# A hybrid pooling and delta-rule decoder trunk on one core: decays made from gate sums that are read back from DRAM, convolution states turned four chunks at a time, queries squared by token

## The chip, the cores and the metric

The kernel runs on one core of a Trainium2 chip, as one launch. The core has a matrix engine (TensorE, PE in the profile; PEld is its loading of weights), a vector engine (VectorE, DVE), a scalar engine (ScalarE, ACT), GpSimd (POOL), and a sync engine (SyncE, SP) that here issues all DMAs. Each engine runs its own instructions in the order in which the program gives them; between engines they wait on semaphores. The metric is the time of one execution in device microseconds; lower is better. The median of three runs counts.

## The reference

Two layers run on a prompt of 512 tokens and on 8 sequences of 8 new tokens (the samples), 576 tokens of 1024 channels in all. Layer 0 mixes tokens by pooling, layer 1 by a gated delta rule; each is followed by a SwiGLU feed-forward block. The change touches the delta-rule mixer alone:

```python
def short_conv(u, buf, w):
    up = jnp.concatenate([buf.astype(u.dtype), u], axis=1)
    out = up[:, 0:L] * w[0]
    for tap in range(1, CONV_WIDTH):
        out = out + up[:, tap:tap + L] * w[tap]
    return jax.nn.silu(out), up[:, L:]
...
    gc = jnp.cumsum(g, axis=-1)
    causal = idx[:, None] >= idx[None, :]
    decay = jnp.exp(jnp.where(causal, gc[..., :, None] - gc[..., None, :], -jnp.inf))
    a_mat = jnp.where(strict, jnp.einsum('bhnid,bhnjd->bhnij', kb, k) * decay, 0.0)
...
    qk = jnp.einsum('bhnid,bhnjd->bhnij', q, k) * decay
...
    q = l2norm(qkv_c[..., :GDN_QK_DIM].reshape(B, L, GDN_K_HEADS, GDN_HEAD_K)) * (GDN_HEAD_K ** -0.5)
    k = l2norm(qkv_c[..., GDN_QK_DIM:2 * GDN_QK_DIM].reshape(B, L, GDN_K_HEADS, GDN_HEAD_K))
```

For each of 16 value heads there is a gate g per token. Its running sum gc inside a chunk gives the decay between two tokens, exp(gc_i - gc_j) for i not before j, and nothing otherwise. Queries and keys (8 heads each, every one shared by two value heads) are scaled by the inverse root of their sum of squares. The convolution takes the last three rows of its input from a state, and gives the last three back as the new state.

## The kernel before

Activations lie with channels on the 128 partitions and tokens along the free dimension; the 576 tokens are handled as halves of 256 and 320. A product with a weight is done in three parts (mm3): weight and activation are split into a rounded part (H, h) and a rest (L, l), and TensorE sums wh x aH, wh x aL and wl x aH. A weight tile comes by DMA into one of three raw buffers (wraw), ScalarE makes wh, and VectorE (or POOL) makes wl.

The prompt is cut into four spans (SPANS) of 128 tokens, and the delta rule works span by span. The 16 value heads are done in four groups G of four. project(G) makes the group's inputs: eight chunks of 128 channels (two of keys, two of queries, four of values), each multiplied by the weights into the banks ps_m, convolved over time (ac, u) and passed through Silu; finish() then turns keys and values to tokens-first with transposes on TensorE, through the single bank ps_x. core(G) makes the decays (QD), the matrices Uw from keys and decays, inverts their 32x32 blocks by a long row of small VectorE products (inv32, tiles ia and ii), combines them, and scans over the spans (scan), braided with the samples' heads (sample_heads). QD has one buffer, so that of group G+1 can be written only when the last matmul of group G's scan has read it. gates(), run once in project(0), makes g for all heads, its split gH and gL, and exponentials of its sums (gce, kde, glp, gls). zproj, zgate and out0 make the output gate and the first half of the output projection, and fill gaps of the groups.

The program is not run in the order in which it is written. The class Plan records all operations with what each depends on, gives each a cost by engine and shape, and searches an order for each engine with a list scheduler, forwards and backwards, in ROUNDS rounds with random stirring from SEED. Operations given to EITHER may go to VectorE or POOL. The scheduler also puts in idle matmuls (ps_w) where it expects TensorE to wait. What it finds is the order in which each engine's instructions are issued; the kernel does not reorder at run time. All DMAs stand in SP's one order, too, and a DMA whose condition is not met holds those behind it.

The decays before, in core(G): for each span, EITHER multiplies the triangle t_le (128x128) by gH and by gL of four heads, into gts (128 x 512 each); TensorE multiplies both by the strict triangle t_gt_r into ps_s, which gives the differences of gate sums; ScalarE takes the exponential of 512 columns into QD; and EITHER multiplies by t_le, to clear the upper part. The squares before: keys are turned to tokens-first and squared on ScalarE with a sum over the free dimension (ksq); queries are squared channels-first in one instruction of 512 columns into u, and TensorE sums each span's 128 columns over the channels with a product by a column of ones. The convolution state before: 24 rows (8 sequences x 3) of four chunks come by DMA, and TensorE transposes each chunk by itself (crow, 24x24; nct on the way back, 27 rows).

## Time and profile before

| What | us |
| --- | --- |
| Median of 3 runs | 1647.77 (1647.66 to 1648.63) |
| The profiled execution | 1655.15 |
| Its span, first to last instruction | 1653.1 |
| TensorE busy in the span | 1610.3 |
| VectorE busy in the span | 1002.9 |
| ScalarE busy in the span | 690.7 |

The profile is of one execution, which took 7.4 us more than the median. Its times are counted from the first instruction. Busy time of an engine is the union of its instructions; on TensorE the instructions overlap, so a matmul's duration is longer than its share of the engine. The delta-rule layer lies about between 500 and 1150 us; before it are the pooling layer and its feed-forward block, behind it the rest of the output projection and the second feed-forward block. A line of a group names engine, operation, output and inputs with shapes; all recorded operations have line 283, so tiles are told apart by their names.

### The profile page before, as it was taken

What the parts mean: (1) busy time and instruction counts of PE and PEld (TensorE: products, weight loads), DVE (VectorE), ACT (ScalarE), POOL (GpSimd) and SP (SyncE); (2) the same over time, 40 slices, a digit from 0 to 9 for tenths busy, and PEclk for the clock granted to TensorE, in tenths of its full rate; (3) what the DMA queues carried; (4) which work ended last, traced back from release to release, by engine and by line L of the source; (5) the groups of instructions that cost most, each with busy time, mean ns of one, the idle gap of its engine ahead of it and who ended that gap; (6) DMA issues with size and microseconds to landing.
All of it is one profiled execution on the core that took longest, in us unless ns stands there. A gap on an engine that the chain in (4) does not pass through costs nothing. (4 is left out here: it accounts for less than half of the span.)

```text
span 1653.1 us, 30697 instructions
## 1 busy us (share of the span) xinstructions
PE 1610.3 (97%) x12421; PEld 1549.2 (94%) x12421; DVE 1002.9 (61%) x2085; ACT 690.7 (42%) x1431; POOL 116.8 (7%) x254
## 2 busy tenths in 40 slices
PE   8999999999999999999999999899999999999998
PEld 8999999999999998898898889789999999999997
DVE  6684213332487898998999899557685312233345
ACT  6654223212355945353463544424464322222244
POOL 4000000000000010021220121100000000000000
PEclk8899999999999999999999999999999999999999
DMA  6245223222366433324333323466644323222333
GB/s 175 74 142 156 78 77 90 88 79 77 93 176 164 119 87 87 100 73 128 96 91 106 109 72 113 159 176 198 203 142 141 90 80 94 78 72 75 101 112 114
DMA packets 329813, 185.27 MB, mean 112 GB/s; under 512 B 12235, under 2 KB 324140, under 8 KB 329407
## 3 DMA queue, kind: packets, MB, share of 16 engines
q1 hardware_dynamic: 329671, 183.30, 38.2%
q8 instruction: 98, 1.61, 0.4%
q14 instruction: 44, 0.36, 0.1%
HBM read 157.73 MB, written 25.77 MB: 111 GB/s over the span
## 5 line engine op out<-in xcount | busy, mean ns | idle before, releaser
L283 DVE TENSOR_TENSOR wl<-wraw,wh 128x1024 fp32r<-128x1024 f32 (+2 forms) x251 | 297.9, 1193 | 279.9 <-PE ps_B L283 88.9
L283 ACT ACTIVATE wh<-wraw 128x1024 fp32r<-128x1024 f32 (+2 forms) x259 | 265.7, 1034 | 470.2 <-PE ps_B L283 212.0
L283 PE MATMUL ps_m<-hH,wh 128*128 128x320 f32 (+1 forms) x832 | 249.1, 312 | 2.1 <-ACT hH L283 0.8
L283 PE MATMUL ps_m<-hL,wh 128*128 128x320 f32 (+1 forms) x832 | 245.4, 307 | 0.0
L283 PE MATMUL ps_m<-hH,wl 128*128 128x320 f32 (+1 forms) x832 | 243.5, 307 | 0.0
L283 PE MATMUL ps_B<-hH,wh 128*128 128x320 f32 x768 | 224.6, 312 | 0.1
L283 PE MATMUL ps_B<-hL,wh 128*128 128x320 f32 x768 | 222.4, 311 | 0.1
L283 PE MATMUL ps_B<-hH,wl 128*128 128x320 f32 x768 | 222.2, 312 | 0.0
L283 PE MATMUL ps_A<-hH,wl 128*128 128x256 f32 x768 | 204.3, 284 | 0.4 <-DVE wl L283 0.2
L283 PE MATMUL ps_A<-hH,wh 128*128 128x256 f32 x768 | 203.4, 284 | 1.2 <-DVE yo L283 1.2
L283 PE MATMUL ps_A<-hL,wh 128*128 128x256 f32 x768 | 203.5, 283 | 0.0
L283 PEld LDWEIGHTS ps_m<-hH,wh 128*128 128x128 f32 x832 | 155.1, 190 | 9.2 <-issue 1.9
L283 PEld LDWEIGHTS ps_m<-hH,wl 128*128 128x128 f32 x832 | 154.6, 190 | 3.8 <-issue 2.0
L283 PEld LDWEIGHTS ps_m<-hL,wh 128*128 128x128 f32 x832 | 155.5, 190 | 2.0
L283 PEld LDWEIGHTS ps_A<-hH,wh 128*128 128x128 f32 x768 | 141.2, 190 | 1.8 <-issue 1.4
L283 PEld LDWEIGHTS ps_A<-hH,wl 128*128 128x128 f32 x768 | 141.4, 190 | 1.4 <-DVE wl L283 1.0
L283 PEld LDWEIGHTS ps_B<-hH,wh 128*128 128x128 f32 x768 | 141.2, 189 | 0.9 <-ACT hH L283 0.3
L283 PEld LDWEIGHTS ps_A<-hL,wh 128*128 128x128 f32 x768 | 141.6, 190 | 0.4 <-DVE hL L283 0.4
L283 PEld LDWEIGHTS ps_B<-hL,wh 128*128 128x128 f32 x768 | 140.7, 189 | 0.4 <-DVE hL L283 0.3
L283 PEld LDWEIGHTS ps_B<-hH,wl 128*128 128x128 f32 x768 | 140.2, 189 | 0.4
L283 PE MATMUL ps_B<-aH,wh 128*128 128x320 f32 x352 | 104.0, 312 | 0.1
L283 PE MATMUL ps_B<-aL,wh 128*128 128x320 f32 x352 | 103.6, 310 | 0.0
(387 smaller groups left out, 3063.1 us busy)
## 6 DMA issues: line engine op xcount, KB each, us to landing
wraw<-in_ffn_w_in_dram SPq DMA_DIRECT2D x112, 512.0 KB
wraw<-in_gdn_w_in_dram SPq DMA_DIRECT2D x56, 512.0 KB
wraw<-in_ffn_w_out_dram SPq DMA_DIRECT2D x48, 448.0 KB
wraw<-in_gdn_w_out_dram SPq DMA_DIRECT2D x24, 512.0 KB
wraw<-in_ffn_w_out_dram SPq DMA_DIRECT2D x16, 512.0 KB
St<-in_state_gdn_rec_dram SPq DMA_DIRECT2D x32, 256.0 KB
out_dram<-St SPq DMA_DIRECT2D x32, 256.0 KB
z_d<-zz SPq DMA_DIRECT2D x16, 288.0 KB
```

The lines of the kernel that those rows point to most:

```text
L283: calls[e](*a, **k)
```

## The change

Four things change.

1. **Decays.** gates() sums the gate along each span for all 16 heads at once, heads on partitions (four matmuls of g with t_le into 16 x 512), copies it (gcr) and stores it to DRAM (gc_d, 32 KB). Per group and span, one DMA reads four heads' rows of it back to all 128 partitions (256 KB into QD); EITHER adds bar, which is -1e30 in the strict triangle and 0 elsewhere; and ScalarE takes four exponentials of 128 columns, one per head, with the negative gate sum of the partition's own token (ngs) as bias. The gts products of the spans, their matmuls and the product with t_le go; gH and gL stay for the samples alone (64 x 16).
2. **Queries squared by token.** Queries are transposed on TensorE like keys, and ScalarE squares each span with a sum into ksq, straight from PSUM. The column sums with ones stay for the samples alone (sqs).
3. **Convolution states.** The 24 rows of four chunks are put below each other on 96 partitions, by four DMAs, and turned with one transpose; on the way back four chunks of 27 rows are turned at once into 108 partitions, and each chunk is stored by two DMAs.
4. **The search.** ROUNDS goes from 46 to 40 and SEED from 4 to 2, and a constant of the cost of small matmuls from 3.2 to 3.9, so the whole order is searched anew.

```diff
@@ -66,7 +66,7 @@
     LEAVE, KEEP = 0.3, 1.0
-    ROUNDS, STIR, SEED = 46, (0.0, 0.0, 300.0, 1000.0, 3000.0), 4
+    ROUNDS, STIR, SEED = 40, (0.0, 0.0, 300.0, 1000.0, 3000.0), 2
@@ -155,7 +155,7 @@
                 if rows == 128:
-                    t = max(t, 220.0) if "tile_position" not in k else max(t / min(3.2, 128 / list(out.ap)[0][1]), 80.0)
+                    t = max(t, 220.0) if "tile_position" not in k else max(t / min(3.9, 128 / list(out.ap)[0][1]), 80.0)
@@ -563,14 +563,16 @@
     z_d = dp.tile([VH, P, T], F32, name="z_d")
+    gc_d = dp.tile([VH, SEQ], F32, name="gc_d")
...
     bet = sp.tile([P, SP1, VH], F32, name="bet")
-    gH = sp.tile([P, SP1, VH], F32R, name="gH")
-    gL = sp.tile([P, SP1, VH], F32R, name="gL")
+    gH = sp.tile([SMP, VH], F32R, name="gH")
+    gL = sp.tile([SMP, VH], F32R, name="gL")
+    ngs = sp.tile([P, SPANS, VH], F32, name="ngs")
@@ -597,8 +599,8 @@
-        t_gt_r = cst.tile([P, P], F32R, name="t_gt_r")
-        DVE.tensor_copy(t_gt_r, t_gt)
+        bar = cst.tile([P, P], F32, name="bar")
+        DVE.tensor_scalar(bar, t_gt, -1e30, None, op0=mult)
@@ -1080,8 +1082,14 @@
                                      op0=mult, op1=mult)
-            DVE.tensor_copy(gH, g)
-            DVE.tensor_tensor(gL, g, gH.bitcast(F32), op=sub)
+            DVE.tensor_copy(gH, g[:SMP, SPANS])
+            DVE.tensor_tensor(gL, g[:SMP, SPANS], gH.bitcast(F32), op=sub)
+            ps = bank("g")[:VH, :SEQ]
+            for s in range(SPANS):
+                PE.matmul(ps[:, s * P:(s + 1) * P], g[:, s], t_le, start=True, stop=True)
+            gcr = cp_.tile([VH, SEQ], F32, name="gcr", tag="T01", bufs=1)
+            ACT.activation(gcr, ps, AF.Copy)
+            SP.dma_start(gc_d, gcr)
@@ -1089,6 +1097,8 @@
                 PE.matmul(ps[:, SPANS], ms, g[:SMP, SPANS], start=True, stop=True)
+                if dst is gce:
+                    ACT.activation(ngs, ps[:, :SPANS], AF.Copy, scale=-1.0)
@@ -1115,21 +1125,20 @@
             out.append((qk, vt, qks, vs, kt))
-            ksq = pp.tile([P, SPANS, 2], F32, name="ksq", tag="ksq", bufs=1)
-            sqs = pp.tile([P, 2, P], F32, name="sqs", tag="sqs", bufs=1)
+            ksq = pp.tile([P, SPANS, 4], F32, name="ksq", tag="ksq", bufs=1)
+            sqs = pp.tile([P, 4, P], F32, name="sqs", tag="sqs", bufs=1)
...
             cp = bank("x")[:, :8 * R0].rearrange("p (c r) -> p c r", c=8)
-            pieces = (((0, KH + 2 * G, 2), (2, 2 * G, 2)), ((0, 2 * KH + 4 * G, 4),))
-            for j4, pc in enumerate(pieces):
-                crow = pp.tile([R0, 4, P], F32, name="crow", tag="nco", bufs=1)
-                for j, i0, n in pc:
-                    SP.dma_start(crow[:, j:j + n].rearrange("r c p -> r (c p)"),
-                                      state_gdn_conv[0].rearrange("b r d -> (b r) d")[:, i0 * P:(i0 + n) * P])
-                for j in range(4):
-                    PE.transpose(cp[:, 4 * j4 + j], crow[:, j], ident[:R0, :R0])
+            for j4 in range(2):
+
+                crow = pp.tile([4 * R0, P], F32, name="crow", tag="crow", bufs=2)
+                for j, (_, _, cc) in enumerate(chunks[4 * j4:4 * j4 + 4]):
+                    SP.dma_start(crow[j * R0:(j + 1) * R0],
+                                 state_gdn_conv[0].rearrange("b r d -> (b r) d")[:, cc * P:(cc + 1) * P])
+                PE.transpose(cp[:, 4 * j4:4 * j4 + 4].rearrange("p c r -> p (c r)"), crow, ident[:4 * R0, :4 * R0])
@@ -1140,7 +1149,7 @@
                 gates()
-            pst, pend = [], []
+            pend = []
@@ -1153,20 +1162,20 @@
                 elif kind == "q":
-                    sq = u
-                    if j == 2:
-                        pst.append(bank("x")[:, :SP1 * 4].rearrange("p (t c) -> p t c", c=4))
-                        for c in range(2):
-                            PE.matmul(pst[0][:, SPANS, c:c + 1], sqs[:, c], ones[:, 0:1], start=True, stop=True)
-                    for tt in range(SP1):
-                        PE.matmul(pst[0][:, tt, j:j + 1], sq[:, tt * P:(tt + 1) * P], ones[:, 0:1], start=True, stop=True)
+                    pv = bank("x", (P, SPANS, P))
+                    for s in range(SPANS):
+                        PE.transpose(pv[:, s], dst[:, s * P:(s + 1) * P], ident)
+                    for s in range(SPANS):
+                        ACT.activation(u[:, s * P:(s + 1) * P], pv[:, s], AF.Square, accum_out=ksq[:, s, 2 + i:3 + i])
                     if j == 3:
+                        pst = bank("x")[:, :4]
+                        for c in range(4):
+                            PE.matmul(pst[:, c:c + 1], sqs[:, c], ones[:, 0:1], start=True, stop=True)
...
                         vt_ = pp.tile([P, 2, SP1, 4], F32, name="rv", tag="rv", bufs=1)
-                        DVE.tensor_scalar(vt_[:, 0, :SPANS, 0:2], ksq, EPS, None, op0=add)
-                        DVE.tensor_scalar(vt_[:, 0, SPANS, 0:2], pst[0][:, SPANS, 0:2], EPS, None, op0=add)
-                        DVE.tensor_scalar(vt_[:, 0, :, 2:4], pst[0][:, :, 2:4], EPS, None, op0=add)
+                        DVE.tensor_scalar(vt_[:, 0, :SPANS], ksq, EPS, None, op0=add)
+                        DVE.tensor_scalar(vt_[:, 0, SPANS], pst, EPS, None, op0=add)
@@ -1217,27 +1226,23 @@
                 ACT.activation(dss.rearrange("p (b t) -> p b t", b=NB), acs, AF.Silu)
-                if kind == "k":
-                    EITHER.tensor_tensor(sqs[:, i].rearrange("p (x t) -> p x t", x=2), dup(dss), dup(dss), op=mult)
-                elif kind == "q":
-                    ACT.activation(u[:, :SEQ], dst, AF.Square)
-                    EITHER.tensor_tensor(u[:, SEQ:].rearrange("p (x t) -> p x t", x=2), dup(dss), dup(dss), op=mult)
+                if kind != "v":
+                    EITHER.tensor_tensor(sqs[:, j].rearrange("p (x t) -> p x t", x=2), dup(dss), dup(dss), op=mult)
...
             R = (CW - 1) * (NB + 1)
-            for j4, pc in enumerate(pieces):
-                nco = pp.tile([R, 4, P], F32, name="nco", tag="nco", bufs=1)
-                pn_ = bank("x", (P, 4, P))
-                for j in range(4):
-                    PE.transpose(pn_[:R, j], nct[:, 4 * j4 + j], ident)
-                ACT.activation(nco, pn_[:R], AF.Copy)
-                for j, i0, n in pc:
-                    src = nco[:, j:j + n].rearrange("r c p -> r (c p)")
-                    SP.dma_start(nc_prompt[0, 0, :, i0 * P:(i0 + n) * P], src[:CW - 1])
-                    SP.dma_start(nc_sample[0].rearrange("b r d -> (b r) d")[:, i0 * P:(i0 + n) * P], src[CW - 1:])
+            nco = pp.tile([4 * R, 2, P], F32, name="nco", tag="nco", bufs=1)
+            pn_ = bank("x", (P, 4, P))[:4 * R, :2]
+            for j4 in range(2):
+                PE.transpose(pn_[:, j4], nct[:, 4 * j4:4 * j4 + 4].rearrange("p c r -> p (c r)"), ident)
+            ACT.activation(nco, pn_, AF.Copy)
+            for j, (_, _, cc) in enumerate(chunks):
+                src = nco[j % 4 * R:(j % 4 + 1) * R, j // 4]
+                SP.dma_start(nc_prompt[0, 0, :, cc * P:(cc + 1) * P], src[:CW - 1])
+                SP.dma_start(nc_sample[0].rearrange("b r d -> (b r) d")[:, cc * P:(cc + 1) * P], src[CW - 1:])
@@ -1275,7 +1280,7 @@
                 EITHER.tensor_tensor(gt, s_le.unsqueeze(1).to_broadcast([SMP, 4, SMP]),
-                                   src[:SMP, SPANS, h4].bitcast(F32).unsqueeze(2).to_broadcast([SMP, 4, SMP]), op=mult)
+                                   src[:, h4].bitcast(F32).unsqueeze(2).to_broadcast([SMP, 4, SMP]), op=mult)
@@ -1482,16 +1487,12 @@
             for s in range(SPANS):
-                ps = bank("s", (P, 4, P))
-                gts = cp_.tile([P, 2, 4, P], F32R, name="gts", tag=("T01", "ia")[s % 2], bufs=1)
-                for i, src in enumerate((gH, gL)):
-                    gt = gts[:, i]
-                    EITHER.tensor_tensor(gt, t_le.unsqueeze(1).to_broadcast([P, 4, P]),
-                                      src[:, s, h4].bitcast(F32).unsqueeze(2).to_broadcast([P, 4, P]), op=mult)
-                    PE.matmul(ps, t_gt_r, gt, start=i == 0, stop=i == 1)
+
                 de = QD[:, :, s]
-                ACT.activation(de, ps, AF.Exp)
-                EITHER.tensor_tensor(de, de, t_le.unsqueeze(1).to_broadcast([P, 4, P]), op=mult)
+                SP.dma_start(de, gc_d[h4, s * P:(s + 1) * P].unsqueeze(0).to_broadcast([P, 4, P]))
+                EITHER.tensor_tensor(de, de, bar.unsqueeze(1).to_broadcast([P, 4, P]), op=add)
+                for h in range(4):
+                    ACT.activation(de[:, h], de[:, h], AF.Exp, bias=ngs[:, s, 4 * G + h:4 * G + h + 1])
...
                 de = QD[:, :, s]

```

Counted over the program's order, TensorE has 11268 instructions before and 11177 after (the idle matmuls go from 90 to 75), VectorE 2087 and 2051, POOL 256 and 256, ScalarE 1316 and 1381 (with loads of tables 34 and 29), SP 481 and 558 DMAs.

On VectorE, where the scan of group 0 ends and the core of group 1 begins, the order before reads as follows (St is the samples' state, S the prompt's, vt the values in which the scan's output is left):

```order
L283 TENSOR_TENSOR gts<-t_le,gL 128x512
L283 TENSOR_TENSOR gts<-t_le,gH 128x512
L283 SCALAR_TENSOR_TENSOR S_1530<-S_1490,glp,ps_s 128x128 x2
L283 TENSOR_TENSOR gts<-t_le,gH 128x512 x2
L283 TENSOR_TENSOR gts<-t_le,gL 128x512 x2
L283 SCALAR_TENSOR_TENSOR vt<-ps_s,rq,t_1512 128x256
L283 TENSOR_TENSOR QD<-QD,t_le 128x4x128 x2
L283 SCALAR_TENSOR_TENSOR Uw<-ps_k,bet,QD 128x128 x4
L283 TENSOR_TENSOR QD<-ps_k,QD 128x2x128 x2
L283 TENSOR_TENSOR gts<-t_le,gH 128x512
L283 SCALAR_TENSOR_TENSOR Uw<-ps_k,bet,QD 128x128 x4
```

and after:

```order
L283 SCALAR_TENSOR_TENSOR S_1524<-S_1484,glp,ps_s 128x128 x2
L283 COPY nct<-u 128x3
L283 COPY nct<-u 128x24
L283 SCALAR_TENSOR_TENSOR vt<-ps_s,rq,t_1506 128x256
L283 TENSOR_TENSOR St<-St,ps_s 128x512
L283 TENSOR_TENSOR gts<-s_le_371,gH 64x256
L283 TENSOR_TENSOR gts<-s_le_371,gL 64x256
L283 TENSOR_TENSOR wl<-wraw,wh 128x1024
L283 SCALAR_TENSOR_TENSOR ac<-u,cwt,ac 128x600
L283 TENSOR_TENSOR QD<-QD,bar 128x4x128
L283 SCALAR_TENSOR_TENSOR ac<-u,cwt,ac 128x600
L283 TENSOR_TENSOR QD<-QD,bar 128x4x128 x2
```

The gts products of the main spans have gone from between the last steps of the scan and QD; the small ones of the samples, a weight split and a product of the convolution have moved there, and the first sum with bar stands behind them.

On SP, at the same place, the order before is (wraw are weights, z_d and nco results on their way out):

```order
L283 DMA wraw<-in_gdn_w_in_dram 128x8x128
L283 DMA out_dram<-St 128x4x128 x4
L283 DMA out_dram<-S_1530 128x2x128
L283 DMA wraw<-in_gdn_w_in_dram 128x8x128 x2
L283 DMA z_d<-zz 128x576
L283 DMA wraw<-in_gdn_w_in_dram 128x8x128 x3
L283 DMA z_d<-zz 128x576
L283 DMA out_dram<-nco 24x256 x2
L283 DMA out_dram<-nco 3x256 x2
```

and after:

```order
L283 DMA wraw<-in_gdn_w_in_dram 128x8x128
L283 DMA out_dram<-St 128x4x128 x2
L283 DMA out_dram<-S_1524 128x2x128
L283 DMA QD<-gc_d 128x4x128 x4
L283 DMA out_dram<-St 128x4x128 x2
L283 DMA wraw<-in_gdn_w_in_dram 128x8x128 x2
L283 DMA z_d<-zz 128x576
L283 DMA wraw<-in_gdn_w_in_dram 128x8x128 x3
L283 DMA z_d<-zz 128x576
L283 DMA wraw<-in_gdn_w_in_dram 128x8x128
L283 DMA out_dram<-nco 3x128 x5
L283 DMA out_dram<-nco 24x128
```

Four loads of QD have come in ahead of the last two stores of St and of the next weights, and the stores of the convolution's new state have become a row of sixteen small ones, of which the first six are shown.

On ScalarE at this place the order before is (jk are squares of the scan's output, u copies of ps_m):

```order
L283 ACT_TABLE_LOAD
L283 ACTIVATE QD<-ps_s 128x4x128 x2
L283 ACTIVATE jk,oss<-vt 128x128 x2
L283 ACTIVATE QD<-ps_s 128x4x128
L283 ACTIVATE u<-ps_m 128x256
L283 ACTIVATE u<-ps_m 128x8x8
L283 ACT_TABLE_LOAD
L283 ACTIVATE oss<-oss,epsd 128x20
L283 ACTIVATE u<-ps_m 128x256
```

and after:

```order
L283 ACT_TABLE_LOAD
L283 ACTIVATE oss<-oss,epsd 128x20
L283 ACT_TABLE_LOAD
L283 ACTIVATE QD<-QD,ngs 128x128 x12
L283 ACTIVATE u<-ps_m 128x256
L283 ACTIVATE u<-ps_m 128x8x8
L283 ACTIVATE QD<-QD,ngs 128x128 x4
L283 ACTIVATE u<-ps_m 128x256
```

The exponentials stood in one-instruction pieces between other work; twelve of the sixteen new ones now stand in one run ahead of the copies of ps_m.

More of the change, by code (lines that the diff above doesn't have):

```diff
@@ L638, in masks @@
         DVE.scalar_tensor_tensor(out=eye2, in0=eyo, scalar=par, in1=eye2, op0=mult, op1=add)
-        return t_gt, t_gt_r, s_le2, s_gt2, s_gt_r, s_in, s_st, eye2
+        return t_gt, bar, s_le2, s_gt2, s_gt_r, s_in, s_st, eye2
     def dup(ap):
@@ L1001, in finish0 @@
                 pre_norm(tp, x, acc2, hi, G_MPRE + NC)
-            t_gt, t_gt_r, s_le2, s_gt2, s_gt_r, s_in, s_st, eye2 = masks(tp)
+            t_gt, bar, s_le2, s_gt2, s_gt_r, s_in, s_st, eye2 = masks(tp)
             s_le = s_le2[:, :SMP]
```

## The prediction

> **What bounds the kernel now.** I read the page first, then a table of the span cut into stages, then the tiles that the change touches, and last the timeline of single stretches.
>
> ```profile
> PE 1610.3 (97%) x12421; PEld 1549.2 (94%) x12421; DVE 1002.9 (61%) x2085; ACT 690.7 (42%) x1431; POOL 116.8 (7%) x254
> PEclk8899999999999999999999999999999999999999
> ```
>
> TensorE counts as busy for 97% of the span, at a granted clock of 0.9 or more after the first two slices. VectorE's 61% is a mean over unlike stages, so I cut the span at the points where the groups of heads change over.
>
> ```profile
> core 0: us, PE busy (x) PEld busy (x) DVE busy (x) ACT busy (x) POOL busy (x), PEclk, DMA share, GB/s
> 0.00:500.00 500.00, 494.41 (x3605) 487.68 (x3606) 235.13 (x442) 197.49 (x359) 26.24 (x86) 0.98 0.38 109
> 500.00:565.00 65.00, 64.14 (x487) 61.16 (x486) 51.23 (x104) 46.64 (x95) 4.21 (x12) 1.00 0.54 150
> 565.00:704.00 139.00, 132.04 (x1085) 120.36 (x1085) 123.49 (x314) 67.44 (x172) 12.86 (x30) 0.99 0.33 94
> 704.00:835.00 131.00, 126.14 (x1071) 114.80 (x1070) 119.34 (x277) 60.66 (x160) 23.81 (x48) 1.00 0.36 101
> 835.00:973.00 138.00, 132.34 (x1114) 120.48 (x1113) 122.92 (x293) 64.23 (x167) 24.32 (x50) 1.00 0.35 99
> 973.00:1060.00 87.00, 78.22 (x687) 72.95 (x685) 74.57 (x172) 44.42 (x93) 17.86 (x20) 0.96 0.42 127
> 1240.00:1653.00 413.00, 405.07 (x3016) 402.21 (x3014) 148.42 (x225) 132.54 (x222) 0.00 (x0) 0.99 0.33 96
> ```
>
> Before 500 us and after 1240 us TensorE is never without work (494 of 500 us, 405 of 413), and the change takes nothing away there. Between 565 and 973 us lie three turns of about 136 us, one for each of the first three groups of heads. There VectorE is busy for 123.49 + 119.34 + 122.92 = 365.75 of 408 us, 90%, and ScalarE for 47%. TensorE holds 1114 matmuls in 138 us there, one in 124 ns, against one in 137 ns at the end of the program; but the turns hold many small ones, so its 96% hides waiting. Both engines are near their limit in the turns, and VectorE is the one that others queue behind at the change-over:
>
> ```profile
> 702.34 0.60 DVE L283 SCALAR_TENSOR_TENSOR S<-S,glp,ps_s 128x128 f32<-128x128 f32 x2
> 702.86 1.29 DVE L283 TENSOR_TENSOR gts<-t_le,gH 128x512 fp32r<-128x512 f32 x2
> 704.06 1.29 DVE L283 TENSOR_TENSOR gts<-t_le,gL 128x512 fp32r<-128x512 f32 x2
> 705.26 0.49 DVE L283 SCALAR_TENSOR_TENSOR vt<-ps_s,rq,t 128x256 f32<-128x256 f32 x1
> ```
>
> No bracket with idle time stands in these rows: VectorE goes from one to the next. Two gts products start 1.20 us before what follows them (702.86 to 704.06, 704.06 to 705.26), so one takes 0.60 us of the engine.
>
> **The decays, on VectorE.** The 32 gts products of the main spans go; the product of QD and t_le becomes a sum with bar of the same shape.
>
> ```profile
> L283 DVE TENSOR_TENSOR gts<-t_le,gH x16: 676/689/781, 545.4 to 973.2; 128x512 fp32r<-128x512 f32 x16
> L283 DVE TENSOR_TENSOR gts<-t_le,gL x16: 677/688/700, 547.0 to 973.8; 128x512 fp32r<-128x512 f32 x16
> L283 ACT ACTIVATE QD<-ps_s x16: 592/599/635, 564.2 to 976.0; 128x512 f32<-128x512 f32 x16
> L283 DVE TENSOR_TENSOR QD<-QD,t_le x16: 673/688/1099, 565.1 to 985.5; 128x512 f32<-128x512 f32 x16
> ```
>
> 32 x 0.60 = **19.2 us less on VectorE**, 4.8 us in each of four groups, all at a place where it is full. What else changes there (shorter gH and gL, four sums fewer in the norms, some small copies taken from or given to POOL) I put at nothing, with 2 us either way.
>
> **The work on TensorE.** Its durations overlap, so I take the distance from one start to the next.
>
> ```profile
> 556.71 0.40 PE L283 MATMUL ps_s<-gts,t_gt_r 128*128 128x512 f32 x1
> 556.95 0.60 PE L283 MATMUL ps_x<-ident,qk 128*128 128x128 f32 x4
> 557.30 0.48 PE L283 MATMUL ps_s<-gts,t_gt_r 128*128 128x512 f32 x1
> ...
> 563.40 1.03 PE L283 MATMUL ps_x<-ones,u 128*128 128x1 f32 x8
> 564.29 0.39 PE L283 MATMUL ps_m<-hL,wh 128*128 128x320 f32 x1
> ...
> 621.44 0.62 PE L283 MATMUL ps_x<-ident,nct 128*27 128x128 f32 x4
> 621.82 0.36 PE L283 MATMUL ps_m<-hH,wh 128*128 128x256 f32 x1
> ...
> 634.90 0.42 PE L283 MATMUL ps_x<-ident,crow 24*128 24x24 f32 x4
> 635.26 0.38 PE L283 MATMUL ps_m<-hH,wh 128*128 128x256 f32 x1
> ```
>
> A gts matmul takes 0.24 us (556.71 to 556.95), four transposes of qk 0.35, eight records of ones,u 0.89 (one column sum is two records), four of nct 0.38, four of crow 0.36. Removed: 32 gts (7.7), 40 column sums (80 records, 8.9), 32 nct (3.0), 32 crow (2.9), together 22.5 us. Added: 32 transposes of the queries (2.8), 8 sums of sqs (16 records at the price of ones,u: 1.8), 8 nct and 8 crow at no less than now (1.5), 4 sums of the gate (8 records: 0.9), together 7.0 us. TensorE has **15.5 us less**. With crow and nct up to twice as dear, since each now carries four chunks, it is 14.0.
>
> **What is added.** The 16 loads of QD carry 256 KB each and have no row yet; the nearest is the load of vt from DRAM, of the same size, out of the same queue:
>
> ```profile
> 774.94 0.53 SPq L283 DMA_DIRECT2D vt<-z_d  x1
> 779.44 0.75 DVE L283 SCALAR_TENSOR_TENSOR vt<-ps_x,prm,vt 128x512 f32<-128x512 f32 x1 [4.87 <-DMA vt<-z_d]
> ```
>
> It took 4.5 us to its user, with a weight tile ahead of it, and VectorE sat idle for 4.87 us meanwhile. A load of QD can be issued only when the last matmul of the group before has read QD, since there is one buffer. What stands on VectorE between that moment and the first sum with bar is, in group 1: a St, two small gts, a wl and a product of the convolution, near 3.3 us (St 0.6, as the gts products of that shape; 2 x 0.41; 1.2; 0.84, less the overlap of about 0.1 that each pair of rows shows). So the first load is 1.2 us late; once per change-over, three times, **3.6 us** (bounds: 0 if it lands in 3.3, and the rival of the serial loads below). In group 0 the norms' short chains lie between, and I count nothing.
>
> ```profile
> L283 DVE SCALAR_TENSOR_TENSOR ac<-u,cwt,ac x96: 824/839/850, 548.8 to 1026.6; 128x600 f32<-128x600 f32 x96
> L283 DVE TENSOR_TENSOR gts<-s_le,gL x3: 408/409/412, 574.4 to 838.3; 64x256 fp32r<-64x256 f32 x3
> L283 DVE TENSOR_TENSOR wl<-wraw,wh 128x1024 fp32r<-128x1024 f32 (+2 forms) x251 | 297.9, 1193 | 279.9 <-PE ps_B L283 88.9
> L283 ACT ACTIVATE u<-kt x32: 293/305/357, 556.2 to 934.7; 128x128 f32<-128x128 f32 x32
> L283 ACT ACTIVATION_READ_ACCUMULATOR u<-kt x32: 185/192/248, 556.4 to 934.9; 128x1 f32 x32
> L283 ACT ACTIVATE u<-qk x8: 613/619/641, 561.2 to 944.9; 128x512 f32<-128x512 f32 x8
> L283 ACT ACTIVATE nh<-yo,prm 128x256 f32<-128x256 f32 x8 | 3.9, 504 | 0.5 <-DVE yo L283 0.4
> L283 SPq DMA_DIRECT2D out_dram<-nco x24: 244/292/722, 622.7 to 1054.2; - x24
> ```
>
> The Trainium skill's page "DMA: Bandwidth & Descriptors", section "Anatomy of one DMA", gives a fixed 2.0 us plus the bytes over 436 GB/s, by which I estimate 2.6 us for 256 KB. By that the load would land under the cover, and the sum below would be -15.2 us, 1632.6. The row above disagrees with its 4.5 us, and the row decides.
>
> Four exponentials of 128 columns, each with its own bias, replace one of 512. One of them lies between 0.31 us (128 columns, no operand by partition) and 0.50 us (256 columns with one); I take 0.40. Four take 1.6 instead of 0.6 us, and the first span of each group is waited for: 4 x 1.0 = **4.0 us** (2.4 to 5.6). The others run beside VectorE's work on Uw. The Trainium skill's page "ScalarE: Activation LUTs", section "What ACT_TABLE_LOAD costs", has 280 ns plus 0.833 ns a column with such a bias, an estimate of 387 ns for 128 columns, by which this term would be 3.8 us and the sum -11.8; no row here has that form.
>
> The squares of the queries grow on ScalarE from 8 x 0.62 to 32 x (0.31 + 0.19) = 16 us, 11 us more over four groups. That engine is idle half of the time in the turns, and the scales that come of it are used by the values, two chunks behind; without that cover a group's last query costs 2.0 us. SP issues 77 more DMAs (481 to 558 by the order), 0.29 us each by the row of the nco stores: 22 us more of a queue whose 481 take 140. The longest run without a weight load is 16 nco stores and 8 crow loads, 24 x 0.29 = 7.0 us. Three raw buffers hold weights for three chunks of 24 x 0.12 + 24 x 0.147 = 6.4 us of matmul each, which hides it; were they empty, it would cost up to 7.0 us a group.
>
> **Sum.** VectorE's relief sets the turns, and TensorE's 15.5 us, being smaller and in the same places, is not added: -19.2 + 3.6 + 4.0 = **-11.6 us**. The profiled execution took 1655.15 us, of which 1653.1 are the span; it becomes 1643.6. The median of the runs shown is 1647.77, 7.4 less than the profiled one; the same step gives **1636.2 us**.
>
> **Rivals.**
> *Both reliefs count*, since a turn is a chain that passes from one engine to the other and waits for neither fully: 19.2 + 15.5 = 34.7, no new wait: 1613.1. Against it: VectorE has only 42 us without work in these 408, so most of TensorE's waiting is for VectorE, and that waiting is relieved once.
> *ScalarE blocks the projections.* Twelve exponentials stand in one run in group 1, ahead of the copies that empty the two ps_m banks. Twelve take 4.8 us, 1.2 more for the late load, less the 1.2 of two old ones: 4.8 us later. Filling a bank takes 24 x 0.12 = 2.9 us, so 1.9 us a change-over reach TensorE, 5.7 in all: 1641.9, up to 1650 if the banks give no cover at all.
> *Slower: the four loads land one after another.* If each takes the 4.5 us of the row for itself, because 128 partitions read the same four rows of DRAM, the last comes after 18 us. VectorE has 3.3 us ahead and, with the sums, Uw and QD of three spans, about 7.3 more; it stalls for 7.4 us in each group, 29.6 in all, against 19.2 - 4.0 gained: +14.4, 1662.2 us. It decides from a stall of 3.8 us a group. Against it: the DMA engines are a third busy in the turns (0.33 to 0.36), so four loads can share them.
> *The change does not take the work away.* The order of instructions excludes it for the counts: TensorE has 32 gts matmuls and 40 column sums in the order of before and none in that of after.
>
> **How the numbers follow.** The whole order is searched anew, which shifts any of these by a few us. Forecast 0.46 (1626 to 1640), the ScalarE rival 0.24 (1640 to 1650, half of it within 0.2%), both reliefs 0.12 (below 1626), serial loads 0.18 (above 1651). Something like 0.2%, 3.3 us, is what a measurement of this kernel can tell from no change: faster 0.46 + 0.12 + 0.12 = 0.70, same 0.12, slower 0.18. A range of 1616 to 1651 leaves out the slow rival and the end of the fast one.
>
> **What would show it.** Right: the three turns become about 132 us long, with VectorE's sum 19 us smaller and its waits for QD loads near 1 us per change-over. ScalarE's rival shows as waits of ps_m matmuls for u just behind the exponentials; the slow one as VectorE waiting several us on QD's loads four times. The forecast is wrong if the turns keep their length with VectorE less busy: then neither engine's work set it, but a chain of waits between them.

## The result, and the profile after

| | Before | After |
| --- | --- | --- |
| Median on one chip, us | 1648.57 (10 runs, 1646.18 to 1653.02) | 1638.62 (10 runs, 1635.39 to 1646.25) |
| Ratio, with its 95% interval | | 0.994 (0.9925 to 0.9955) |
| The profiled execution, us | 1655.15 | 1638.33 |
| Its span, us | 1653.1 | 1636.5 |

The changed kernel is faster by 0.6%, 9.9 us (7.4 to 12.4). The two profiled executions differ by more, 16.8 us, and the first thing to learn from them is where that surplus lies. On the page after, the sums of busy time and the clock by slices read:

```profile
PE 1590.0 (97%) x12287; PEld 1533.0 (94%) x12287; DVE 983.8 (60%) x2049; ACT 699.4 (43%) x1528; POOL 115.4 (7%) x254
PEclk9999999999999999999999999899999999999998
```

VectorE has 19.1 us less, the 32 gts products; TensorE 20.3, idle matmuls among it. The clock row starts with 9s where before had two 8s, and ends on an 8. The first 50 us of both, before ahead of after, in the view by windows (columns: window, its length, busy time and instructions of PE, PEld, DVE, ACT, POOL, then granted clock, DMA share, GB/s):

```profile
0.00:50.00 50.00, 45.13 (x251) 42.01 (x252) 32.93 (x86) 32.92 (x80) 19.02 (x78) 0.78 0.55 145
0.00:50.00 50.00, 45.00 (x301) 41.81 (x302) 35.62 (x94) 36.96 (x91) 18.70 (x78) 0.93 0.54 145
```

TensorE was busy equally long, but at a clock of 0.78 it got through 251 matmuls, against 301 at 0.93. This is the lower layer's stretch, which the change does not touch. To cut it off, I mark the beginning of the delta-rule layer by the first matmul into ps_e, and its end by the first sg of the feed-forward behind it. Before and then after, from the rows of these tiles (the last two columns of times are first and last start):

```profile
L283 PE MATMUL ps_e<-hH,wh x64: 278/283/523, 496.0 to 525.6; 128*128 128x256 f32 x64
L283 ACT ACTIVATE sg<-ps_A x2: 383/384/385, 1215.2 to 1217.9; 128x256 f32<-128x256 f32 x2
L283 PE MATMUL ps_e<-hH,wh x64: 278/283/364, 486.0 to 515.7; 128*128 128x256 f32 x64
L283 ACT ACTIVATE sg<-ps_A x5: 365/372/386, 1198.8 to 1223.4; 128x256 f32<-128x256 f32 x5
```

The layer takes 1215.2 - 496.0 = 719.2 us before and 1198.8 - 486.0 = 712.8 after, so 6.4 us less. 10.0 us of the difference lie ahead of it, and 0.2 behind it. Only the 6.4 can belong to the change. A span compared without such a cut would have credited it with 16.6. The clock differs inside the layer, too: by windows from mark to mark it is 0.99 before and 0.98 after.

Inside the layer I mark each group by its first Uw: 580.4, 707.0, 840.6, 976.5 before, and 567.8, 693.8, 826.5, 956.5 after. From the layer's start to the first Uw the change gains 2.6 us (84.4 to 81.8), over the three turns 7.4 (396.1 to 388.7), and in the last stage, from the last Uw to the layer's end, it **loses** 3.6 (238.7 to 242.3). The turns in the view by windows, cut to whole us, each time the three turns and their sum, before and then after:

```profile
580.00:707.00 127.00, 120.19 (x1000) 109.00 (x999) 114.56 (x282) 54.15 (x151) 12.86 (x26) 0.99 0.33 94
707.00:841.00 134.00, 129.14 (x1095) 117.76 (x1093) 122.35 (x286) 64.96 (x168) 25.45 (x49) 1.00 0.36 100
841.00:976.00 135.00, 129.34 (x1092) 117.49 (x1091) 119.92 (x283) 61.30 (x159) 23.26 (x50) 1.00 0.35 99
sum 396.00, PE 378.67 PEld 344.25 DVE 356.84 ACT 180.41 POOL 61.56; mean PE 126.22 PEld 114.75 DVE 118.95 ACT 60.14 POOL 20.52
```

```profile
568.00:694.00 126.00, 121.12 (x1021) 110.58 (x1020) 114.72 (x276) 67.69 (x189) 14.57 (x32) 1.00 0.39 110
694.00:826.00 132.00, 124.36 (x1031) 114.13 (x1030) 114.97 (x277) 63.20 (x184) 24.51 (x44) 0.96 0.38 106
826.00:956.00 130.00, 126.05 (x1057) 115.00 (x1056) 116.92 (x276) 63.43 (x188) 21.32 (x49) 0.99 0.38 107
sum 388.00, PE 371.53 PEld 339.71 DVE 346.60 ACT 194.31 POOL 60.40; mean PE 123.84 PEld 113.24 DVE 115.53 ACT 64.77 POOL 20.13
```

VectorE's busy time in these windows falls by 10.2 us, and their length by 8. What VectorE has idle in their sum hardly changes: 396 - 356.84 = 39.2 us before, 388 - 346.60 = 41.4 after. So in these two executions the sum of the turns shrinks with VectorE's work. The single turns do not follow it: by the first Uw they shorten by 0.6, 0.9 and 5.9 us, with VectorE's work 0.2 us up, 7.4 down and 3.0 down. The second, where the work fell most, ran at a clock of 0.96 after. Of VectorE's 19.1 us, counted from mark to mark, 9.6 lie in the turns, 6.2 between the layer's start and the first Uw, 1.1 in the last stage and 2.2 ahead of the layer.

The new operations, in the rows of the tile QD after (minimum, median, maximum in ns; the last row is idle time ahead of a sum with bar, in us and times):

```profile
L283 ACT ACTIVATE QD<-QD,ngs x64: 385/389/427, 566.3 to 962.6; 128x128 f32<-128x128 f32 x64
L283 SPq DMA_DIRECT2D QD<-gc_d x16: 364/506/1208, 558.7 to 951.0; - x16
L283 DVE TENSOR_TENSOR QD<-QD,bar x16: 673/684/695, 563.4 to 958.8; 128x512 f32<-128x512 f32 x16
...
  DMA QD<-gc_d: 2.7, 4
```

VectorE waited 2.7 us for the loads in all. The change-over to group 1 in the timeline, VectorE, SP and ScalarE (start, duration, instruction, how many in a row):

```profile
687.45 2.02 SPq L283 DMA_DIRECT2D QD<-gc_d  x4
690.26 0.83 DVE L283 SCALAR_TENSOR_TENSOR ac<-u,cwt,ac 128x600 f32<-128x600 f32 x1
691.21 0.69 DVE L283 TENSOR_TENSOR QD<-QD,bar 128x512 f32<-128x512 f32 x1
692.58 1.29 DVE L283 TENSOR_TENSOR QD<-QD,bar 128x512 f32<-128x512 f32 x2
...
692.52 3.63 ACT L283 ACTIVATE QD<-QD,ngs 128x128 f32<-128x128 f32 x12
```

The four loads are issued in 2.0 us, and the first sum begins 3.76 us after the first issue, 0.1 us behind the convolution product that covers it. Twelve exponentials run in 3.63 us, so they follow each other at 0.29 to 0.30 us ((3.63 - 0.39)/11 = 0.295), though one lasts 0.39: they overlap. The Trainium skill's page "ScalarE: Activation LUTs", section "What ACT_TABLE_LOAD costs", says that activations behind one another overlap by about 93 ns; the rows agree with 0.389 - 0.295 = 94 ns.

The loss in the last stage stands in the chain that ended last. First SP's rows of the timeline before, then after, and then pieces of the chain after:

```profile
1046.29 3.50 SPq L283 DMA_DIRECT2D out_dram<-nco  x4
1050.88 0.36 SPq L283 DMA_DIRECT2D og<-og_d  x1
```

```profile
1024.56 2.60 SPq L283 DMA_DIRECT2D og<-og_d  x3
1033.44 5.21 SPq L283 DMA_DIRECT2D out_dram<-nco  x15
1038.75 0.36 SPq L283 DMA_DIRECT2D og<-og_d  x1
```

```profile
1033.03 0.39 ACT nco L283
1033.44 0.28 SPq L283
...
1038.75 2.79 DMA og<-og_d
1041.56 0.42 ACT hH L283
1042.01 0.42 DVE hL L283
1042.43 0.35 DVE ve L283
```

The load of og, an input of the output projection, stands in SP's order behind the last group's stores of nco. SP waits with them until ScalarE has made nco (1033.4), then issues fifteen, one in 0.35 us (5.21/15), and only then the load. ScalarE, in its own order, holds hH of og, and behind it VectorE's ve and TensorE's next product wait. TensorE stands idle for 3.16 us ahead of it:

```profile
1042.91 1.19 PE L283 MATMUL ps_s<-ve,kt 128*128 128x256 f32 x2 [3.16 <-DVE ve L283]
```

### The profile page after: what moved, and what is told of

It is laid out like the page before. It is cut to its first block, busy times and chain, and to the rows that moved or that the text cites. A ratio compares the mean times of both kernels' runs of the same rounds, so it can differ in the third digit from the quotient of the medians.

```text
span 1636.5 us, 30622 instructions
## 1 busy us (share of the span) xinstructions
PE 1590.0 (97%) x12287; PEld 1533.0 (94%) x12287; DVE 983.8 (60%) x2049; ACT 699.4 (43%) x1528; POOL 115.4 (7%) x254
## 5 line engine op out<-in xcount | busy, mean ns | idle before, releaser
L283 PE MATMUL ps_m<-hH,wl 128*128 128x320 f32 (+1 forms) x832 | 244.6, 311 | 0.0
L283 PE MATMUL ps_B<-hL,wh 128*128 128x320 f32 x768 | 218.8, 311 | 0.1
L283 PE MATMUL ps_B<-hH,wh 128*128 128x320 f32 x768 | 218.8, 311 | 0.0
L283 PE MATMUL ps_B<-hH,wl 128*128 128x320 f32 x768 | 218.5, 311 | 0.3 <-DVE wl L283 0.2
L283 PE MATMUL ps_B<-aH,wl 128*128 128x320 f32 x352 | 100.8, 311 | 0.0
```

Source lines behind the costliest of these rows:

```text
L283: calls[e](*a, **k)
```

## The experiments

Three theories were to be told apart. **V**: VectorE's relief sets the length of the turns, as predicted. **T**: TensorE's relief does, and VectorE's counts little. **S**: the search drew a better order, and the operations taken away do not matter. Ratios are to the kernel before on the same chip. "Layer" is the length marked above, in one profiled execution each, and "turns" that from the first Uw to the fourth group's.

| Kernel | Ratio (95% interval) | Layer, us | Turns, us |
| --- | --- | --- | --- |
| before | 1 | 719.2 | 396.1 |
| after | 0.994 (0.9925 to 0.9955) | 712.8 | 388.7 |
| e1_search: before, new search | 1.0019 (1.0 to 1.0037) | 728.1 | 399.6 |
| e2_old_search: the change, old search | 1.0022 (1.0008 to 1.0037) | 719.7 | 392.1 |
| e3_decays: decays alone, new search | 0.9972 (0.9953 to 0.9991) | 715.6 | 394.0 |
| e4_rest: queries and states alone, new search | 1.0069 (1.0041 to 1.0096) | 728.8 | 405.1 |
| f1_vector_back: after, VectorE +19 us | 1.0055 (1.0034 to 1.0077) | 732.9 | 407.6 |
| f2_tensor_back: after, TensorE +14 us | 0.9975 (0.9959 to 0.999) | 721.9 | 394.8 |
| f3_late_stores: after, stores behind og | 0.9917 (0.9894 to 0.9941) | 710.3 | 390.9 |
| f4_loads_twice: after, serial loads | 1.0233 (1.0207 to 1.0259) | 761.7 | 420.9 |
| g1_before_s7: before, seed 7 | 1.0058 (1.0037 to 1.0078) | 726.4 | 396.9 |
| g2_after_s7: the change, seed 7 | 0.9996 (0.9978 to 1.0014) | 718.2 | 391.3 |
| g3_before_s11: before, seed 11 | 1.0099 (1.0077 to 1.0121) | 730.8 | 394.7 |
| g4_after_s11: the change, seed 11 | 1.0017 (1.0003 to 1.003) | 723.4 | 400.9 |

### The change taken apart: e1 to e4

e1 is the kernel before with nothing but the constants of the search:

```diff
-    ROUNDS, STIR, SEED = 46, (0.0, 0.0, 300.0, 1000.0, 3000.0), 4
+    ROUNDS, STIR, SEED = 40, (0.0, 0.0, 300.0, 1000.0, 3000.0), 2
...
-min(3.2, 128 / list(out.ap)[0][1])
+min(3.9, 128 / list(out.ap)[0][1])
```

> The kernel before with the new ROUNDS, SEED and cost constant alone; nothing of the work changes. Theory V (VectorE's relief sets the turns) and theory T (TensorE's relief does): no gain but what a newly searched order happens to give, 1648.6 us plus or minus 4. Theory S (the gain is that of the newly drawn order): 1639, as the whole change.

e2 is the whole change with these two lines left as they were.

> The whole change in decays, queries and states, with ROUNDS 46, SEED 4 and 3.2 as before. Theories V and T: 1638.6 us plus or minus 4. Theory S: near 1648.6.

e3 has these two lines and the parts of the diff on gates(), masks and QD; e4 has them and the parts on crow, nco, ksq and sqs.

> The decays alone, with the new search; queries and states as before. Theory V: all 19.2 us of VectorE's relief are here, and all the waits for loads, so the whole gain: 1636 to 1640 us. Theory T: of TensorE's 15.5 us only 7.7 - 0.9 = 6.8 are here, so 6.8/15.5 of 10 us: about 1644.

> Queries and states alone, with the new search; decays as before. Theory V: VectorE keeps its gts products, so no gain: 1648.6 us plus or minus 4, or 2 to 3 more where the sixteen stores in a row hold up loads behind them (5.2 us of SP's queue in the last group of the profile after). Theory T: 8.7 us of TensorE's work are here: 1643.

The new constants alone make the kernel before no faster (1.0019), so the gain is not the constants'. But with the old ones the change gains nothing either (1.0022). With the new constants the change is worth 0.994 - 1.0019, -0.8%; with the old +0.2%. Decays alone give -0.5% against e1, the rest +0.5%, both together -0.8%: the parts do not add up. Put on the 1648.6 us of the kernel before, e1 stands at 1651.7, e2 at 1652.2, e3 at 1644.0 and e4 at 1659.9. Only e1 is where V expected it. e2 is nearer to what S expected (1648.6) than to V's and T's 1638.6, e3 is at T's 1644, and e4 is above what any of them said. Each of these kernels has an order drawn for itself, and the draw is as large as what is to be measured. So the next runs kept the order still.

### The order kept, one cost put back: f1 and f2

f1 and f2 take the order that the search found for the changed kernel, and put one thing into it twice, after the search. f1 makes 16 of the weight splits wl between the first and the last load of QD twice on VectorE; f2 runs the 32 products of queries and keys into ps_k twice on TensorE. Both repeat work that is done anyway.

```diff
-            for i, e in best[1]:
+            for i, e in self.edit(best[1]):
...
+        twice = set((mine[::2] + mine[1::8])[:16])
+        seq = [x for p, x in enumerate(seq) for _ in range(2 if p in twice else 1)]
```

> The kernel after, in its own searched order, with 16 weight rests (wl, VectorE, 1.19 us each, 1.12 from start to start) between the first and the last load of QD made twice: 18 us of VectorE's work put back, with nothing for TensorE and nothing in the chain of the decays. Theory V: most of it comes back, 12 to 18 us: 1651 to 1657 us. Theory T: VectorE's idle time in the turns (42 us) takes it: under 5 us, below 1644.

> The kernel after, in its own order, with the 32 products of keys with keys and queries (two records of 0.215 us each) made twice: 13.8 us of TensorE's work put back. Theory V: TensorE waits for VectorE there anyhow, so less than half comes back: below 1645 us. Theory T: nearly all comes back: 1650 to 1653.

f1 is 1.0055 - 0.994 = 0.0115 above the changed kernel, 19 us (give or take 4, from both intervals). f2 is 0.0035 above it, 5.8 us (give or take 3.6), of 13.8 put back (64 records, 0.215 us from one start to the next). The turns of f1, and the sum over the turns of f2, by windows:

```profile
571.00:704.00 133.00, 122.54 (x1014) 111.35 (x1013) 122.67 (x283) 66.72 (x187) 15.25 (x32) 0.99 0.37 103
704.00:843.00 139.00, 125.78 (x1041) 114.83 (x1041) 120.78 (x282) 64.32 (x188) 25.34 (x44) 0.96 0.37 103
843.00:979.00 136.00, 127.44 (x1060) 115.49 (x1059) 122.39 (x281) 64.13 (x190) 22.77 (x50) 0.99 0.37 104
sum 408.00, PE 375.77 PEld 341.67 DVE 365.85 ACT 195.18 POOL 63.35; mean PE 125.26 PEld 113.89 DVE 121.95 ACT 65.06 POOL 21.12
```

```profile
sum 395.00, PE 378.09 PEld 344.78 DVE 346.90 ACT 195.31 POOL 60.30; mean PE 126.03 PEld 114.93 DVE 115.64 ACT 65.10 POOL 20.10
```

In f1 VectorE is busy for 365.85 us, 19.2 more than after, and the turns are 20 us longer by these windows (18.9 by the first Uw, 407.6 against 388.7); its idle time is 42.2 us, against 41.4. In this order, VectorE's work passes into the time nearly one for one. Put on the 1648.6 us, f1 is at 1657.6, just above V's range. Not all of it need be waiting: the executions of f1 had a mean granted clock of 0.983, those of the changed kernel 0.987. I estimate that this is worth at most 0.004 of the time, 6.5 us; the other 12 are still more than T allows. In f2 VectorE is as busy as after, and idle for 48.1 us: TensorE's work is paid for in part, 0.42 of it (0.16 to 0.68 by the interval). f2 tells the price of products that VectorE's Uw waits for, and not of TensorE's work at other places. T falls by both runs, and in this order V's rate is right, as far as adding a cost tells what removing one is worth.

### The stores behind the load: f3

In the same kept order, the sixteen stores of nco of the last group are issued behind the eighth load of og.

```diff
+        seq = [x for p, x in enumerate(seq[:last + 1]) if p not in st] + [seq[p] for p in st] + \
+            [x for p, x in enumerate(seq) if p > last and p not in st]
```

> The kernel after, in its own order, but the sixteen stores of the convolution's state in the last group are issued behind the eight loads of og instead of ahead of the last ones. If the stores stand on the path there (they take 5.2 us of SP's queue, and the matmul behind the load of og waits for 3.2 to 3.5 us): 2 to 5 us less, 1634 to 1637. If the load is needed later than that anyhow: no change, 1638.6.

SP's rows of the timeline:

```profile
1027.59 2.56 SPq L283 DMA_DIRECT2D og<-og_d  x3
...
1038.10 0.34 SPq L283 DMA_DIRECT2D og<-og_d  x1
1038.49 5.55 SPq L283 DMA_DIRECT2D out_dram<-nco  x16
```

The three loads ahead come 3.0 us later here than after (1027.59 against 1024.56), the load in question 0.65 us sooner (1038.10 against 1038.75): beside its surroundings it gains 3.7 us. It no longer stands behind the stores, and in place of TensorE's 3.16 us its wait for ve is 1.1. ScalarE's waits for og fall from 11.4 to 7.1 us. The last stage takes 237.8 us, against 242.3 after and 238.7 before: the loss there is made good. f1 and f2, which leave the stores where they stand after, take 242.5 and 244.6.

The granted clock moves with it. These are 30 us around the late load, from about 70 us behind the last group's first Uw, before, after and in f3 (third number from the end):

```profile
1046.00:1076.00 30.00, 26.60 (x213) 22.98 (x210) 16.28 (x36) 10.96 (x30) 1.25 (x1) 0.89 0.38 122
1026.00:1056.00 30.00, 21.59 (x175) 17.20 (x174) 13.85 (x34) 10.55 (x32) 1.25 (x1) 0.77 0.46 144
1031.00:1061.00 30.00, 23.52 (x198) 19.11 (x199) 17.36 (x42) 9.74 (x30) 2.48 (x3) 0.89 0.44 137
```

By these rows I estimate that the lower clock alone can cost up to 30 x 0.12 = 3.6 us, as much as the stage lost. Whether the late load brought the clock down is not shown, so the 3.6 lost and the 4.5 gained back are prices of the wait and the clock together. The ratio of 0.9917 is the lowest of all kernels here, 3.8 us under the changed one, but the two intervals overlap (0.9894 to 0.9941, 0.9925 to 0.9955), so the stage's rows show the gain more surely than the times do.

### The loads made serial: f4

In the kept order each load of QD is issued twice, and since both write the same buffer, the copy waits until the first has landed.

```diff
+        twice = {p for p, (i, e) in enumerate(seq) if e == "SP" and whose(i, e).startswith("QD")}
```

> The kernel after, in its own order, with each of the 16 loads of QD issued twice, so that the sums with bar wait for twice the bytes. If loads of QD share the DMA engines (forecast's view): the last of eight lands 2 to 4 us later, half of it covered, 3 to 6 us in all: 1641 to 1645. If each takes 4.5 us for itself (the rival): 18 us more per group, above 1680.

SP's row at the change-over to group 1, two of VectorE's sums there, and the waits for all loads:

```profile
703.23 17.02 SPq L283 DMA_DIRECT2D QD<-gc_d  x8
...
710.24 0.69 DVE L283 TENSOR_TENSOR QD<-QD,bar 128x512 f32<-128x512 f32 x1 [3.37 <-DMA QD<-gc_d]
714.82 0.69 DVE L283 TENSOR_TENSOR QD<-QD,bar 128x512 f32<-128x512 f32 x1 [3.13 <-DMA QD<-gc_d]
...
  DMA QD<-gc_d: 49.6, 16
```

The loads now come one after the other, and VectorE stalls at every one; in this group its sums stand 4.3 to 4.6 us apart. The stalls are 49.6 us in all, and the layer is 48.9 us longer, but its granted clock also fell, to 0.95 from 0.98, so that the two figures need not be the same thing. Put on the 1648.6 us, f4 is at 1687.0, above the 1680 of the rival: the edit puts the loads in a row, so that it could not test the 1641 to 1645 of loads that share. It is the rival of the serial loads, made real: where after lets four loads share the DMA engines, the rival would have cost 48 us (1.0233 - 0.994), and not the 29.6 of stalls that the prediction gave it. That is a price from above, as each load shares the engines with the copy of the one before, and as the clock is in it.

### Two more draws of both kernels: g1 to g4

Both kernels with the changed constants and two other seeds:

```diff
-    ROUNDS, STIR, SEED = 40, (0.0, 0.0, 300.0, 1000.0, 3000.0), 2
+    ROUNDS, STIR, SEED = 40, (0.0, 0.0, 300.0, 1000.0, 3000.0), 7
```

> The kernel before with its order drawn anew: the search's constants of the change (40 rounds, 3.9), but seed 7. Theory V: between 0.997 and 1.004 of the kernel before, since only the draw differs (the two draws so far gave 1.000 and 1.0019). Theory S: anywhere from 0.992 to 1.004, as often as not as fast as the changed kernel.

> The whole change with the same draw's constants, seed 7. Theory V: 8 to 14 us (0.5 to 0.8%) under the kernel before at seed 7, give or take 4 us for each draw. Theory S: over or under it with like chances, and the four pairs (old search, new search, seed 7, seed 11) have a mean near nothing.

> The kernel before with the search's constants of the change but seed 11. Theory V: 0.997 to 1.004 of the kernel before. Theory S: 0.992 to 1.004.

> The whole change with seed 11. Theory V: 8 to 14 us under the kernel before at seed 11, give or take 4 us for each draw. Theory S: over or under it with like chances.

| Draw | Before | Changed | Difference |
| --- | --- | --- | --- |
| 46 rounds, 3.2, seed 4 | 1 | 1.0022 | +0.2%, +3.6 us |
| 40 rounds, 3.9, seed 2 | 1.0019 | 0.994 | -0.8%, -13.0 us |
| 40 rounds, 3.9, seed 7 | 1.0058 | 0.9996 | -0.6%, -10.2 us |
| 40 rounds, 3.9, seed 11 | 1.0099 | 1.0017 | -0.8%, -13.5 us |

Both new pairs fell into the 8 to 14 us that V expected. The expectation that V and S shared was wrong: redrawn, the kernel before stood 0.6 and 1.0% above itself, outside 0.997 to 1.004 and 0.992 to 1.004. The four kernels of either kind lie 16 and 14 us apart, more than the change is worth. The mean of the four differences is -8.3 us; their spread (+3.6 to -13.5) is too wide for four pairs alone to rule out a mean of nothing. Against S speaks f1, where the order was the same and VectorE's work alone cost nearly its own length; it does not say how much of the 9.9 us is the draw's.

The profiled executions of the eight kernels also tell whether VectorE's idle time stays, before and then changed, by windows from mark to mark:

| Draw | VectorE busy in the layer, us | VectorE idle in the layer, us | VectorE idle in the turns, us |
| --- | --- | --- | --- |
| 46 rounds, 3.2, seed 4 | 601.2, 584.4 | 118.0, 135.3 | 39.2, 50.2 |
| 40 rounds, 3.9, seed 2 | 601.7, 584.3 | 126.5, 128.5 | 41.3, 41.4 |
| 40 rounds, 3.9, seed 7 | 602.7, 582.4 | 123.8, 135.8 | 39.3, 47.9 |
| 40 rounds, 3.9, seed 11 | 601.3, 586.9 | 129.5, 136.5 | 42.8, 50.4 |

It stayed only in the draw that the changed kernel has. In the mean of the four, VectorE has 17.2 us less to do in the layer, is idle for 9.6 us more, and the layer is 7.6 us shorter: less than half of the relief became time. VectorE's idle time ahead of vt, whose load from z_d comes through SP's order as well, rises in the mean from 12.8 to 18.0 us (11.7, 14.7, 10.2 and 14.4 before; 18.5, 14.0, 16.4 and 22.9 changed; whole executions), and 2.5 to 4.4 us ahead of the sums with bar are new. These two make up most of the 9.6; why vt's loads come later is not shown. With the old constants the layer keeps its length (719.2 and 719.7) though VectorE has 17 us less to do in it, and the turns shorten by 4.0 us with 15.0 less: this comes close to the prediction's own sign of being wrong, a chain of waits that sets the time. With seed 11 the turns even grow, from 394.7 to 400.9. Why the draws differ so much is not shown.

## Why the prediction was right, and where it was off

The forecast was 1636.2 us and faster; the median is 1638.62. The relief was sized as -11.6 us and measured as -9.9 (7.4 to 12.4).

- **VectorE's relief of 19.2 us sets the turns.** The sum of its busy time fell by 19.1. f1 shows the rule for work put back into the order of the changed kernel, 19 us for 19.2. For work taken away and the order searched anew it is not shown: the idle time of the turns stayed in one draw of four, and in the mean of the four less than half of the relief became time. In the draw at hand the turns shortened by 7.4 us, by 0.6, 0.9 and 5.9 and not by 4 each, since VectorE's work in them fell by 10.2 us and not by 14.4, as the new order has other work there.
- **TensorE's relief is not added.** Wrong in size: f2 puts the price of TensorE's work at its place at 5.8 of 13.8 us, 0.4 for one, and not nothing. By that rate, an estimate for work at other places, the 15.5 us would be worth about 6.5. It was one term left out of the sum, and the reason given for it, that the waiting is relieved once, holds for a bit more than half.
- **The late loads, 3.6 us.** Measured 2.7 in four waits, and 2.5 to 4.4 in the other draws. The first sum began 3.76 us after the issue where the row of vt had given 4.5. The cover was 3.6 us at the change-over to group 1, where the prediction said 3.3 and its own terms, with 0.1 taken off between neighbours, add up to 3.1. The 2.6 us that it set beside this, from the Trainium skill's page "DMA: Bandwidth & Descriptors", section "Anatomy of one DMA — SWDGE (gpsimd) path", belong by that heading to DMAs issued by GpSimd; here SP issues them. What the prediction left out is the load of vt: VectorE's idle time ahead of it went from 11.7 to 14.0 us, and in the mean of the draws up by 5.2.
- **Four exponentials, 4.0 us.** One takes 0.389 us, as put (0.40), but the step that took four times 0.40 was wrong, since they overlap and follow each other at 0.295. Four then end 3 x 0.295 + 0.389 = 1.27 us after the first began, 0.67 more than the old one, 2.7 us over four groups. How much of it stands on the path is not shown; VectorE waited for the exponentials once, for 0.7 us.
- **ScalarE blocks the projections.** Twelve exponentials did stand in one run, but it lasted 3.63 us, not 4.8. In the whole execution the matmuls into ps_m waited 2.1 us for u, 1.6 more than before, and their weight loads 3.4, 1.8 more; not the 5.7 more of the rival.
- **The small stores are hidden.** This step failed in the last group. It looked for weight loads behind the stores, for which three raw buffers give cover, and not for other loads. SP issued 5.3 us of stores ahead of a load of og, 3.7 of them at its cost by f3's rows; the last stage lost 3.6 us against before, and f3 gets back 4.5, in both with a change of the clock that may be part of it.
- **The new search shifts this by a few us.** Too small: four draws of one kernel lie 14 to 16 us apart. The draw in the changed kernel is the best of its four, as that before is of its own. Best against best is -9.9 us, the mean against the mean -8.3.

With the terms as they were found the sum reads -19.2 - 6.5 + 2.7 + 2.7 + 3.6 = -16.7 us. The layer got 6.4 us shorter in the one profiled execution, and the medians 9.9. In the rows of the layer, VectorE's work fell by 16.9 us and its idle time grew by 10.5: 3.5 ahead of the first Uw, 2.2 in the turns, 4.7 in the last stage. The granted clock is in it, too: 0.98 against 0.99 over the layer, where a hundredth of 713 us is an estimated 7 us at most. How the rest divides between waits, clock and draw is not shown. So that 1636.2 came within 2.4 us of 1638.6 is in part luck: the terms come out at -16.7 when they are mended, and the other three draws of the changed kernel stand 9 to 14 us higher. That the squares by token and the turned states bring anything by themselves stays open: e4 differs from e1 by +0.5%, but these are two draws. Serial loads were no danger as issued, and f4 says what they would have been.

## What to carry to other kernels

Ask of the engine with the least idle time in a stretch whether its idle time stays as its work changes, and ask it in more than one order; where it stays, its work is worth its length, and the other engine's only a part. Count its waits for every load in the stretch, not only for the new ones, and read the granted clock of a stage beside its length. Where a change also redraws a searched order, compare several draws of both kernels or keep the order and put a cost back: one pair measures the draw as much as the change. And when stores are cut into smaller ones on an in-order queue, look at every load behind them, in every group, the last above all.

## What the runs showed of the hardware

Four loads of 256 KB, each reading the same 2 KB for 128 partitions, shared the DMA engines instead of queueing: at the change-over to group 1 the third sum had ended 6.4 us after the first issue (692.58 + 1.29 - 687.45), where loads that wait for their turn (f4) let the sums follow each other in 4.3 to 4.6 us. While they ran, with two stores of St and a weight tile issued right behind them, the windows of after show the engines full.

```profile
692.00:693.00 1.00, 1.00 (x9) 0.73 (x7) 1.00 (x2) 0.99 (x3) 0.00 (x0) 1.00 1.11 318
693.00:694.00 1.00, 1.00 (x9) 1.00 (x9) 1.00 (x3) 1.00 (x4) 0.88 (x1) 1.00 1.17 348
```

The DMA share (second number from the end) is above 1 there and the rate 318 and 348 GB/s, for the loads and what runs beside them together. And the issue of a small store takes SP 0.27 to 0.30 us where it carries 1.5 KB (3 rows) and 0.30 to 0.36 where it carries 12 KB (24 rows), by the sixteen rows of the last group: eight times the bytes cost a third more at most. So the sixteen stores of a group, six before, hold the queue by their number more than by their bytes.
